# A decoder block on one core: x on the load queue, the first w_in tiles after modulation set 0, and the S5 constants begun during x

## The chip, the core and the metric

The kernel runs on one core of a Trainium2 chip. Five engines work beside each other: TensorE (PE, whose weight loads are listed apart as PEld), VectorE (DVE), ScalarE (ACT), GpSimd (POOL) and SyncE (SP), which here only issues loads. The metric is the device time of one launch in microseconds (us). Times of several launches and the trace of one profiled launch are given; in the trace every time counts from the start of its span.

## What is computed

```python
mod = silu(c) @ W_ada + b_ada           # 6 vectors: shift1, scale1, gate1, shift2, scale2, gate2
h = rms(x, norm1_w) * (1 + scale1) + shift1
u, q, k, v = split(h @ W_in)            # 256 rows of 2048; W_in has 4096 columns
y_ssm = s5_mixer(u, ...)                # 64 groups, exp/cos/sin of a*dt, a scan over 256 rows, GELU, GLU
y_att = dilated_attention(q, k, v, ...) # three branches with ALiBi, merged
x = x + gate1 * (concat(y_ssm, y_att) @ W_out)
h2 = rms(x, norm2_w) * (1 + scale2) + shift2
x = x + gate2 * ((silu(h2 @ W_gate) * (h2 @ W_up)) @ W_down)
```

x is 256 x 2048 in fp32, c one row of 2048. All weights are fp32.

## The kernel before, in words

**Weights.** Every weight tile is 128 x 1024 fp32 (0.52 MB). `load` (line 108) issues it on SP into the ring `raw`, which has 6 slots. For the matmuls on activations `ahead` (line 126) makes two tiles of it: `whi`, a copy in the reduced matmul type, cast by ACT (line 135), and `wlo`, what the cast lost, subtracted by DVE (line 137). A product takes three passes: whi with both halves of the activation and wlo with its upper half. There are 3 slots of whi and 3 of wlo (NHL = 3).

**The early stage** runs from the start to about 165 us and mixes four streams, one small step of each at a time, in the loop over `n` at the end of the printed code:

- `ada` makes the modulation vectors. Each of its first 8 sets makes two columns of shift1 and scale1 in two steps of four wada tiles: two tiles in the `raw` ring and a pair, `rawp`, in a buffer of its own. After a set ACT copies the sum (`adaev`), PE turns it into columns (`adac`, line 212), DVE makes `sh1` and `g1` (lines 216 and 218) of it, and `make_h` makes `htmp` and `hT` (lines 623 and 626) on DVE and ACT.
- `x_norm` transposes x on PE through the accumulators `uacc0` and `uacc1` (line 343) in two halves, copies them out as `xT` (line 349, one by ACT, one by DVE), squares x on ACT (line 346), and makes 1/rms on DVE and PE (line 360).
- `s5_consts` makes the constants of the SSM, well over a hundred short VectorE operations, most on 128 x 32 numbers. After it come `ssm_rot` and `ssm_tables` (four tables, m0 to m3), on DVE, ACT, PE (`wtp`, `pk`, `pk2`: lines 577, 583 and 587) and POOL.
- `unit` is the first part of h @ W_in. Unit p takes two columns of hT (set p) with three win tiles: two for u (line 639, into uacc0 and uacc1) and one for q (line 154).

**What sets the order.** SP's instructions stand in the written order. On the other engines a scheduler places the instructions; those of `make_h`, `adac` and the casts have high priority. `next(st_)` is called at steps 0 to 8, and goes through x_norm with one step of s5_consts each time; from step 9 on, `tab_step` spends a budget of 1.2 per step on what is left of `st_` and then on the tables. `ahead(NHL)` loads the first three win tiles at n == 8; after that a unit loads the next tile each time it takes one. At n == 10 SP issues `bct` (1 MB, used by the last part of the S5 constants).

ACT's queue issues `smt` (0.19 MB of small constants, among them the identity for the transposes), then x0 and x1, the halves of x (1 MB each).

Of the kernel before, what the change touches and what calls it, by code (L numbers as in the profile page):

```python
# [61 lines left out]
def body(tc, sm, tabs, bc, brow, x, wada, wg2, win, wglu, wout, wgate, wup, wdown, out):  # L62
    nc = tc.nc
    V, A, PE, G, SP = nc.vector, nc.scalar, nc.tensor, nc.gpsimd, nc.sync
# [19 lines left out]
    A.dma_start(smt, sm)  # L84
    xt = [xp.tile([128, D], F32, name=f"x{t}", tag="x", bufs=2) for t in range(2)]
    for t in range(2):
        A.dma_start(xt[t], x[t])
    col = lambda n: smt[:, COLS[n][0]:COLS[n][1]]
    ident = col("id")
    ones = const.tile([128, 128], F32, name="ones")  # L90
# [34 lines left out]
    def ahead(n, place=None):  # L125
        while len(ready) < n and order:
            raw = load(order.pop())
            if place:
                hl = place([128, 2, 2, 512], "whl", F32R)
                hi, lo = hl[:, 0], hl[:, 1]  # L130
            else:
                hi = ring.tile([128, 2, 512], F32R, name="whi", bufs=NHL)
                lo = ring.tile([128, 2, 512], F32R, name="wlo", bufs=NHL)
            with tc.high_priority(offset=HP):
                A.copy(hi, raw)  # L135
            with tc.high_priority(offset=HP2):
                V.tensor_tensor(out=lo, in0=raw, in1=hi.bitcast(F32), op=ALU.subtract)  # L137
            ready.append((hi, lo))
# [195 lines left out]
    def x_norm():  # L334

        ss1 = p1.tile([128, 2], F32, name="ss1")
        for h in range(2):
            xn = P8([128, 8, 256], f"xT{h}")
            for t in range(2):
                for i in range(2):  # L340
                    for k in range(4):
                        kc = h * 8 + i * 4 + k
                        PE.transpose(uacc[i][:, k, t * 128:(t + 1) * 128], xt[t][:, kc * 128:(kc + 1) * 128], ident)
                if h == 0:
                    junk = P8([128, D], "junk")
                    A.activation(junk, xt[t], AF.Square, accum_out=ss1[:, t:t + 1])
                    yield
            for i in range(2):
                (V.tensor_copy if i else A.copy)(xn[:, 4 * i:4 * i + 4], uacc[i])
            xnT.append(xn)  # L350
            yield
            if h == 0:
                with tc.high_priority(offset=HH):
                    V.tensor_scalar(out=ss1, in0=ss1, scalar1=1.0 / D, scalar2=EPS, op0=ALU.mult, op1=ALU.add)
                    rs1 = rsqrt(p1, ss1, 2, "a")
                    rb = ms([128, 256], "rb")
                    for t in range(2):
                        dg = T2([128, 128], "dgx")
                        V.tensor_scalar(out=dg, in0=ident, scalar1=rs1[:, t:t + 1], scalar2=None, op0=ALU.mult)
                        PE.matmul(rb[:, t * 128:t * 128 + 128], lhsT=ones, rhs=dg, start=True, stop=True)  # L360
                    A.copy(rsx, rb)
                yield
# [288 lines left out]
    def unit():  # L651
        while units:
            try:
                next(units[0])
                return
            except StopIteration:
                units.pop(0)

    def start():
        a, b = x_norm(), s5_consts()  # L660
        while next(a, 0) is None:
            next(b, None)
            yield
        yield
        yield from b

    def tabs_early():
        yield from st_
        for m in range(NTAB):
# [4 lines left out]
            yield from ssm_tables(m)  # L674

    st_ = start()
    tab_gen = tabs_early()
    U_ = []
# [13 lines left out]
    def tab_step(budget):  # L692
        debt[0] = max(debt[0] - budget, -budget)
        if debt[0] < 0:
            c_ = next(tab_gen, None)
            debt[0] += c_ or 0.0

    work = 0.0
    for n in range(66):
        next(ada)  # L700
        if n == NBC:
            SP.dma_start(bct.rearrange("p a b c -> p (a b c)"), bc)
        if n < 9:
            next(st_)
        else:
            tab_step(TB)
        if n == 8:
            ahead(NHL)
        if n >= U0:
            work += RATE  # L710
            while work >= 1.0:
                unit()
                work -= 1.0
# [548 lines left out]
def program(arrays):  # L1262
    import concourse.bacc as bacc
    nc = bacc.Bacc("TRN2", target_bir_lowering=False, num_devices=1)
    aps = {k: nc.dram_tensor(k, v.shape, F32, kind="ExternalInput").ap() for k, v in arrays.items()}
    out = nc.dram_tensor("out", (2, 128, D), F32, kind="ExternalOutput").ap()
    with tile.TileContext(nc) as tc:
        body(tc, out=out, **aps)
    return nc
# [8 lines left out]
```

## Time and profile before

| | us |
|---|---|
| launches (three) | 1246.68, 1247.48, 1251.21 |
| median | 1247.48 |
| the profiled launch | 1248.12 |
| its span in the trace | 1246.3 |
| PE busy in the span | 1193.3 (96%) |
| DVE busy | 793.3 (64%) |
| ACT busy | 572.2 (46%) |
| chain that ended last | PE 79%, DVE 10%, DMA 5%, ACT 3% |

The profiled launch is 1.82 us longer than its span. The page cuts the span into 40 slices of 31 us and gives the busy share of each engine in tenths. Here are the lines of PE, DVE, the clock that TensorE was granted and the DMA engines:

```profile
PE   4789899999998999899999999999999999999998
DVE  7964766477879998855665565565555444545544
PEclk9899999999999999899999999999999999999999
DMA  9889878897996899367777777777766656666662
```

The first column is the first 31 us. PE is below 9 tenths in four of the first five slices and in three later ones, and otherwise busy nearly all the time.

### The profile page before, as it was taken

The numbers are of one execution on the slowest core, as the hardware profiler recorded it, in microseconds if no ns is written. First come the engines' busy times: TensorE is split into PE (matmuls) and PEld (weight loads), VectorE is DVE, ScalarE is ACT, GpSimd is POOL, SyncE is SP. The second block draws the span as 40 slices with busy tenths as digits, with TensorE's granted clock in tenths as the row PEclk, the third lists the DMA queues.
The fourth block names the chain that finished last, engine by engine and source line by source line (L and its number), as shares of the span: only waits on it lengthen the run. The fifth ranks groups of instructions, "written<-read, shape, count | busy, mean of one in ns | idle before, by whom it ended". The sixth has DMA issues, their size and how long they took to land.

```text
span 1246.3 us, 17021 instructions
## 1 busy us (share of the span) xinstructions
PE 1193.3 (96%) x6312; PEld 954.0 (77%) x6312; DVE 793.3 (64%) x1402; ACT 572.2 (46%) x871; POOL 50.5 (4%) x90
## 2 busy tenths in 40 slices
PE   4789899999998999899999999999999999999998
PEld 2567667667797777688888888888888878888886
DVE  7964766477879998855665565565555444545544
ACT  3654574456455445644444444444444443434332
POOL 1110001121120000000000000000000000000000
PEclk9899999999999999899999999999999999999999
DMA  9889878897996899367777777777766656666662
GB/s 378 314 289 365 311 265 293 287 305 265 327 318 205 300 338 338 120 212 241 233 241 224 240 241 241 230 228 248 236 187 187 197 161 199 207 197 205 197 208 67
DMA packets 93906, 306.85 MB, mean 246 GB/s; under 512 B 18080, under 2 KB 20544, under 8 KB 93184
## 3 DMA queue, kind: packets, MB, share of 16 engines
q1 hardware_dynamic: 80784, 294.69, 70.7%
q0 software_dynamic: 11312, 6.70, 2.7%
q10 hardware_dynamic: 1728, 4.38, 0.9%
q8 instruction: 49, 0.80, 0.3%
q14 instruction: 33, 0.27, 0.1%
HBM read 301.54 MB, written 4.19 MB: 245 GB/s over the span
## 4 chain that ended last, share of the span: by engine, by line
PE 79%; DVE 10%; DMA 5%; ACT 3%; issue 2%; POOL 0%; DVEq 0%; ACTq 0%; POOLq 0%
PE ff L154 38%; PE dn L154 14%; PE qkv L154 8%; PE dnl L154 5%; PE ada L255 3%; DMA raw<-wada 3%; DVE wlo L137 2%; PE uacc L639 2%; PE wo L154 2%; DMA raw<-win 1%; PE y L763 1%; PE S L733 1%; DVE gate L292 1%; PE q L154 1%; DVE wkt L368 1%
## 5 line engine op out<-in xcount | busy, mean ns | idle before, releaser
L137 DVE TENSOR_TENSOR wlo<-raw,whi 128x1024 fp32r<-128x1024 f32 x365 | 446.6, 1224 | 334.5 <-ACT whi L135 333.8
L135 ACT CAST whi<-raw 128x1024 fp32r<-128x1024 f32 x365 | 384.8, 1056 | 499.3 <-PE ff L154 270.1
L154 PE MATMUL ff<-whi,h2T 128*128 128x512 f32 x1408 | 438.5, 391 | 0.7 <-DVE h2T L1074 0.5
L154 PEld LDWEIGHTS ff<-whi,h2T 128*128 128x128 f32 x1408 | 264.6, 188 | 56.6 <-ACT h2T L1073 1.0
L154 PE MATMUL ff<-wlo,h2T 128*128 128x512 f32 x704 | 274.5, 390 | 0.0
L154 PE MATMUL dn<-whi,aT 128*128 128x512 f32 x528 | 163.4, 390 | 0.0
L154 PEld LDWEIGHTS ff<-wlo,h2T 128*128 128x128 f32 x704 | 132.5, 188 | 26.9
L154 PEld LDWEIGHTS dn<-whi,aT 128*128 128x128 f32 x528 | 99.1, 188 | 21.0 <-ACT whi L135 0.2
L154 PE MATMUL qkv<-whi,hT 128*128 128x512 f32 x320 | 108.1, 405 | 0.3 <-ACT whi L135 0.2
L154 PE MATMUL dn<-wlo,aT 128*128 128x512 f32 x264 | 103.1, 391 | 0.0
L154 PEld LDWEIGHTS qkv<-whi,hT 128*128 128x128 f32 x320 | 60.6, 190 | 25.5 <-issue 6.4
L154 PE MATMUL qkv<-wlo,hT 128*128 128x512 f32 x160 | 64.1, 401 | 2.0 <-DVE wlo L137 2.0
L1132 DVE SCALAR_TENSOR_TENSOR gate<-raw,cs,gate 128x1024 f32<-128x1024 f32 x32 | 41.1, 1284 | 38.3 <-DMA raw<-wg 38.3
L639 PE MATMUL uacc<-hT,whi 128*128 128x256 f32 x256 | 51.7, 299 | 6.9 <-ACT whi L135 6.9
L154 PEld LDWEIGHTS dn<-wlo,aT 128*128 128x128 f32 x264 | 49.6, 188 | 10.8 <-issue 0.5
L154 PE MATMUL dnl<-whi,aT 128*128 128x512 f32 x176 | 54.4, 389 | 0.0
L292 DVE SCALAR_TENSOR_TENSOR gate<-raw,cs,gate 128x512 f32<-128x512 f32 x64 | 48.0, 754 | 7.6 <-DMA raw<-wada 7.2
L639 PEld LDWEIGHTS uacc<-hT,whi 128*128 128x128 f32 x256 | 42.0, 201 | 13.5 <-ACT whi L135 9.9
L255 PE MATMUL ada<-raw,c 128*4 128x256 f32 (+1 forms) x496 | 50.7, 492 | 0.0
L639 PE MATMUL uacc<-hT,wlo 128*128 128x256 f32 x128 | 38.7, 302 | 5.7 <-DVE wlo L137 5.7
L154 PEld LDWEIGHTS dnl<-whi,aT 128*128 128x128 f32 x176 | 33.0, 188 | 7.0 <-DVE o L368 0.2
L154 PEld LDWEIGHTS qkv<-wlo,hT 128*128 128x128 f32 x160 | 30.5, 191 | 8.9 <-DVE wlo L137 2.3
(318 smaller groups left out, 1257.1 us busy)
## 6 DMA issues: line engine op xcount, KB each, us to landing
raw<-wada SPq DMA_DIRECT2D x130, 512.0 KB, 5.3
raw<-wgate SPq DMA_DIRECT2D x88, 512.0 KB, 4.3
raw<-wup SPq DMA_DIRECT2D x88, 512.0 KB, 4.1
raw<-wdown SPq DMA_DIRECT2D x88, 512.0 KB, 3.7
raw<-win SPq DMA_DIRECT2D x64, 512.0 KB, 5.5
raw<-wout SPq DMA_DIRECT2D x32, 512.0 KB, 4.9
raw<-wg SPq DMA_DIRECT2D x32, 512.0 KB, 4.0
rawp<-wada SPq DMA_DIRECT2D x30, 512.0 KB, 7.2
```

Of the source, the lines that this page charges most:

```text
L135: A.copy(hi, raw)
L137: V.tensor_tensor(out=lo, in0=raw, in1=hi.bitcast(F32), op=ALU.subtract)
L154: PE.matmul(ps[t] if type(ps) is list else ps[:, t], lhsT=lhs(a, t), rhs=w[:, j], start=first and n == 0, stop=last and n == 2)
L255: PE.matmul(ps[32 * q:32 * q + 4, 0:w], lhsT=c7[:, kc, 3 - i:7 - i], rhs=wts[t][:, j * w:(j + 1) * w], start=q not in seen, stop=n == len( ...
L292: V.scalar_tensor_tensor(out=gb, in0=wt[:, j], scalar=cs[:, 2 * h + j:2 * h + j + 1], in1=gb, op0=ALU.mult, op1=ALU.add)
L368: V.tensor_tensor(out=o, in0=a, in1=b, op=op)
L639: PE.matmul(uacc[b][:, c], lhsT=wt[:, j, w], rhs=h[:, j, a], start=(kc == 0 and n == 0 and c % 2 == 0), stop=(kc == 15 and n == 2), skip_g ...
L733: PE.matmul(S[:, e, Q], lhsT=wv[:, 0, Q, e].rearrange("p i c -> p (i c)"), rhs=U[:, m, Q], start=True, stop=True)
L763: PE.matmul(y[:, Q], lhsT=Vt[:, Q, e].rearrange("p r c -> p (r c)"), rhs=hp[:, e, Q], start=False, stop=e == 1, skip_group_check=True)
L1132: V.scalar_tensor_tensor(out=g, in0=wt, scalar=cs[:, k:k + 1], in1=g, op0=ALU.mult, op1=ALU.add)
```

## The change

It moves the two loads of x from ACT's queue to the head of SP's, ahead of all weights; it calls `ahead(NHL)` at n == 4 in place of n == 8; and `start` takes two, two and one steps of s5_consts in its first three calls and none in the next six, with the rest of them from n == 9 on in `tab_step`.

```diff
     for t in range(2):
-        A.dma_start(xt[t], x[t])
+        SP.dma_start(xt[t], x[t])
@@
     def start():
         a, b = x_norm(), s5_consts()
-        while next(a, 0) is None:
-            next(b, None)
+        for i in range(9):
+            next(a, None)
+            for _ in range((2, 2, 1)[i] if i < 3 else 0):
+                next(b, None)
             yield
-        yield
         yield from b
@@
             tab_step(TB)
-        if n == 8:
+        if n == 4:
             ahead(NHL)
```

**SP, from the first wada tile on.** `raw` and `rawp` with wada are ada's tiles (four in a step, two steps in a set), those with win the tiles of unit 0. Before:

```order
L110 DMA raw_124<-wada 128x1024
L249 DMA rawp_126<-wada 128x1024 x2
L110 DMA raw_249<-wada 128x1024
L110 DMA raw_251<-wada 128x1024
L249 DMA rawp_253<-wada 128x1024 x2
L110 DMA raw_332<-wada 128x1024
L110 DMA raw_334<-wada 128x1024
L249 DMA rawp_336<-wada 128x1024 x2
L110 DMA raw_385<-win 128x1024
L110 DMA raw_391<-win 128x1024
L110 DMA raw_397<-win 128x1024
L702 DMA bct_117<-bc 128x2048
```

And now, from the head of the queue:

```order
L87 DMA x0_77<-x 128x2048
L87 DMA x1_78<-x 128x2048
L110 DMA raw_122<-wada 128x1024
L110 DMA raw_124<-wada 128x1024
L249 DMA rawp_126<-wada 128x1024 x2
L110 DMA raw_262<-wada 128x1024
L110 DMA raw_264<-wada 128x1024
L249 DMA rawp_266<-wada 128x1024 x2
L110 DMA raw_304<-win 128x1024
L110 DMA raw_310<-win 128x1024
L110 DMA raw_316<-win 128x1024
L110 DMA raw_324<-wada 128x1024
```

The three win tiles now stand ahead of set 1's first step (raw_324 and on), where they stood behind it (raw_332 to rawp_336), and bct, which followed the win tiles, follows that step. x stands ahead of everything.

**DVE, at set 0's columns.** `wlo` is unit 0's, `te` and `wkr` are the running products of the S5 constants, ss_ and el their small operands, `sh1` and `g1` the modulation columns of set 0. Before:

```order
L216 TENSOR_TENSOR sh1_103<-adac_403,smt_75 128x2
L216 TENSOR_TENSOR g1_102<-adac_403,smt_75 128x2
L368 TENSOR_TENSOR ss_td_113<-el_116 128x32
L368 TENSOR_TENSOR ss_dt_107<-el_116 128x32
L218 SCALAR_TENSOR_TENSOR g1_102<-g1_102,smt_75 128x2
L368 TENSOR_TENSOR ss_ard_108<-el_116 128x32
L371 TENSOR_SCALAR el_116<-ss_td_113 128x32
L623 SCALAR_TENSOR_TENSOR htmp_410<-xT0_146,g1_102,rsx_106 128x256 x2
L368 TENSOR_TENSOR el_116<-ss_ard_108,ss_dt_107 128x32
L371 TENSOR_SCALAR ss_tb_111<-pw_114 128x32
L368 TENSOR_TENSOR wkr_494<-te_493,el_116 128x16
L626 SCALAR_TENSOR_TENSOR hT_409<-htmp_410,sh1_103,hT_409 128x256 x2
```

Now:

```order
L368 TENSOR_TENSOR wkr_549<-te_548,el_116 128x16x16 x2
L137 TENSOR_TENSOR wlo_307<-raw_304,whi_306 128x1024
L368 TENSOR_TENSOR te_548<-wkr_549 128x8x16
L137 TENSOR_TENSOR wlo_313<-raw_310,whi_312 128x1024
L216 TENSOR_TENSOR sh1_103<-adac_347,smt_75 128x2
L216 TENSOR_TENSOR g1_102<-adac_347,smt_75 128x2
L368 TENSOR_TENSOR te_548<-wkr_549 128x8x16
L218 SCALAR_TENSOR_TENSOR g1_102<-g1_102,smt_75 128x2
L137 TENSOR_TENSOR wlo_319<-raw_316,whi_318 128x1024
L623 SCALAR_TENSOR_TENSOR htmp_354<-xT0_146,g1_102,rsx_106 128x256 x2
L368 TENSOR_TENSOR wkr_549<-te_548,el_116 128x512
L626 SCALAR_TENSOR_TENSOR hT_353<-htmp_354,sh1_103,hT_353 128x256 x2
```

Before, sh1 to hT stood in the middle of the S5 constants and ahead of every wlo. Now nearly all the S5 constants and the three wlo stand ahead of hT, and only bct follows.

**PE, at the end of unit 3 and set 4's columns.** uacc is unit 3's u part, q00 and q01 its q part, `adac_1274` the columns of set 4, on which unit 4 waits. Before:

```order
L639 MATMUL uacc1_119<-hT_847,wlo_1172 128x256
L154 MATMUL q00_120<-whi_1233,hT_847 128x512
L154 MATMUL q01_121<-whi_1233,hT_847 128x512
L212 MATMUL adac_1274<-sel_100,adaev_1243 128x2 x2
L154 MATMUL q00_120<-wlo_1234,hT_847 128x512
L154 MATMUL q00_120<-whi_1233,hT_847 128x512
L154 MATMUL q01_121<-wlo_1234,hT_847 128x512
L154 MATMUL q01_121<-whi_1233,hT_847 128x512
```

Now:

```order
L154 MATMUL q00_120<-wlo_1195,hT_784 128x512
L154 MATMUL q00_120<-whi_1194,hT_784 128x512
L154 MATMUL q01_121<-whi_1194,hT_784 128x512
L583 MATMUL pk_1218<-wst_1157,te_920 32x128 x8
L154 MATMUL q01_121<-wlo_1195,hT_784 128x512
L154 MATMUL q01_121<-whi_1194,hT_784 128x512
L587 MATMUL pk2_1228<-smt_75,te_920 128x128
L212 MATMUL adac_1274<-sel_100,adaev_1204 128x2 x2
L255 MATMUL ada_98<-rawp_1246,c7_92 4x256 x8
L255 MATMUL ada_98<-raw_1244,c7_92 4x256 x4
L255 MATMUL ada_98<-raw_1242,c7_92 4x256 x4
```

The q tile's matmuls, which followed adac_1274, now precede it, with table m3's `wtp`, `pk` and `pk2` among them. From there on both programs have the same order on PE.

## Rows read from the trace of the kernel before

**Rows 1.** Windows: us, busy us of PE, PEld, DVE, ACT, POOL (instructions), PEclk, DMA share, GB/s.

```profile
10.00:15.00 5.00, 1.94 (x8) 1.57 (x8) 4.89 (x39) 3.01 (x3) 0.95 (x1) 1.00 1.00 408
...
50.00:55.00 5.00, 4.47 (x52) 2.05 (x52) 4.80 (x16) 4.59 (x9) 0.00 (x0) 0.66 0.53 206
...
70.00:75.00 5.00, 4.33 (x46) 2.46 (x46) 5.00 (x16) 3.78 (x8) 0.00 (x0) 1.00 0.78 269
...
95.00:130.00 35.00, 34.58 (x351) 26.99 (x353) 19.30 (x56) 16.05 (x34) 1.95 (x6) 1.00 0.98 384
...
400.00:1246.00 846.00, 835.84 (x3719) 686.19 (x3717) 504.65 (x542) 361.17 (x405) 1.08 (x2) 1.00 0.68 219
```

**Rows 2.** Timeline, first 22 us: start, us, engine, line, operation, [idle before <- releaser].

```profile
5.31 0.22 ACT L182 ACTIVATE cs<-smt 128x16 f32<-128x16 f32 x1 [2.36 <-DMA smt<-sm]
...
10.22 1.91 ACT L346 ACTIVATE junk<-x 128x2048 f32<-128x2048 f32 x1 [4.70 <-DMA x<-x]
...
14.00 1.91 ACT L346 ACTIVATE junk<-x 128x2048 f32<-128x2048 f32 x1 [1.76 <-DMA x<-x]
...
15.07 1.89 PE L255 MATMUL ada<-rawp,c 128*4 128x256 f32 x16 [2.79 <-DVE ss_tb L371]
...
18.59 1.97 PE L343 MATMUL uacc<-smt,x 128*128 128x128 f32 x8
...
20.60 1.23 DVE L349 COPY xT<-uacc 128x1024 f32<-128x1024 f32 x1 [3.56 <-PE uacc L343]
...
21.88 1.75 PE L343 MATMUL uacc<-smt,x 128*128 128x128 f32 x14 [1.32 <-DVE xT L349]
```

**Rows 3.** Timeline, VectorE, 27 to 40 us.

```profile
29.64 0.88 DVE L626 SCALAR_TENSOR_TENSOR hT<-htmp,sh,hT 128x256 fp32r<-128x256 f32 x2
...
33.09 1.22 DVE L137 TENSOR_TENSOR wlo<-raw,whi 128x1024 fp32r<-128x1024 f32 x1
...
38.90 0.42 DVE L371 TENSOR_SCALAR bct<-bct 128x512 f32<-128x512 f32 x1
```

**Rows 4.** Timeline, TensorE, 34 to 58 us.

```profile
34.36 0.58 PE L639 MATMUL uacc<-hT,wlo 128*128 128x256 f32 x1 [2.87 <-DVE wlo L137]
...
45.05 1.05 PE L255 MATMUL ada<-raw,c 128*4 128x256 f32 x16
...
48.21 0.61 PE L212 MATMUL adac<-sel,adaev 128*128 128x2 f32 x4 [2.11 <-ACT adaev L267]
...
57.19 0.36 PE L639 MATMUL uacc<-hT,wlo 128*128 128x256 f32 x1
```

**Rows 5.** Timeline, TensorE, 75 to 123 us.

```profile
75.64 0.38 PE L639 MATMUL uacc<-hT,wlo 128*128 128x256 f32 x1 [0.26 <-DVE wlo L137]
...
94.77 0.66 PE L577 MATMUL wtp<-smt,wst 128*128 128x128 f32 x4 [0.44 <-ACT wv L578]
...
95.18 0.36 PE L639 MATMUL uacc<-hT,wlo 128*128 128x256 f32 x1
...
97.27 0.65 PE L583 MATMUL pk<-wst,te 128*32 128x128 f32 x16
...
104.13 0.50 PE L212 MATMUL adac<-sel,adaev 128*128 128x2 f32 x4
...
106.99 1.05 PE L255 MATMUL ada<-rawp,c 128*4 128x256 f32 x16
...
109.17 0.27 PE L639 MATMUL uacc<-hT,wlo 128*128 128x256 f32 x1
...
122.61 0.50 PE L639 MATMUL uacc<-hT,whi 128*128 128x256 f32 x2
```

**Rows 6.** Timeline, ScalarE and TensorE, 120 to 141 us.

```profile
120.47 1.05 ACT L135 CAST whi<-raw 128x1024 fp32r<-128x1024 f32 x1 [2.50 <-DMA raw<-win]
...
132.38 0.50 PE L154 MATMUL q<-wlo,hT 128*128 128x512 f32 x1 [0.81 <-DVE wlo L137]
...
140.18 0.50 PE L639 MATMUL uacc<-hT,whi 128*128 128x256 f32 x2 [1.16 <-ACT whi L135]
```

## What is forecast, before the changed kernel has run

> **What bounds the kernel now.** I read the shares first, then windows, then the timeline of the early stage, engine by engine. From 400 us on TensorE is busy for 835.84 of 846 us [rows 1]. Nothing the change touches is there: whatever the early stage wins or loses is carried to the end, unless a wait in between swallows it. The DMA engines are full between 95 and 130 us (share 0.98, 384 GB/s) but not before: 0.53 at 50 to 55 us, 0.78 at 70 to 75 us [rows 1]. So the question is when the early stage hands over at about 130 us, and who is late there.
>
> In the first 40 us the late one is VectorE: busy 4.89 of 5 us at 10 to 15 us, in 39 operations, so 0.125 us each [rows 1]. It makes the S5 constants, and sh, g, hT and wlo must fit in between. TensorE waited 2.87 us for the first wlo (34.36 us) [rows 4]. VectorE's one large hole is 3.56 us ahead of its first copy of transposed x at 20.60 us [rows 2]: the second half of x, squared from 14.00 us on, was transposed behind ada's first step, which began at 15.07 us, so these eight transposes ran at 18.59 us only.
>
> **Part by part: x on SP.** The small constants stay at the head of ACT's queue and x leaves it. At 408 GB/s [rows 1] x's 2.1 MB take 5.1 us. By 15.07 us 4.8 MB had come (smt, x, four wada tiles and some of dct), 11.7 us at that rate, so bytes flow from about 3.3 us. Behind smt and a share of dct, x0 is there by about 7.3 us and x1 by about 9.9 us, against 10.22 and 14.00 us [rows 2]. The same bytes stand ahead of ada's first step, so that still has its tiles near 15 us and gains nothing.
>
> The sixteen transposes of the first half run as soon as x lands, and VectorE's first xT copy starts at about 14 to 15 us instead of 20.60. The hole of 3.56 us goes. But the second half's transposes wait for these copies to free uacc: 16 of them, at 1.97/8 = 0.246 us when the engine came from idling and 1.75/14 = 0.125 us otherwise [rows 2], so 2.0 to 3.9 us; VectorE meets its second xT copy after 26 short operations (3.2 us) and waits there 0.6 to 1.2 us. I take a lead of 2.5 us for VectorE from there on; the bounds are 3.56 (no new wait) and 1.6 (a new wait of 2.0, all the transposes at the slow price).
>
> smt gates the first work of both ACT and VectorE; it landed at 5.31 us [rows 2]. Its bound is from there to 7.3 us (behind all of x0): 0 to +2.0. I take 0, its own row. By the Trainium skill ("DMA: Bandwidth & Descriptors", section "Queues, rings and completion order") each DMA engine goes round the queues that it has work for, one packet at a time; x's 8 KB rows now stand on the other queue in place of wada's 4 KB rows, so by that page smt would get fewer turns and land later. No row of before shows it; it is a rival below.
>
> **The S5 constants and the win tiles.** By the order, the three wlo and hT of unit 0 now stand behind nearly all S5 constants. Before, these constants ended at 38.90 us [rows 3], with everything of unit 0 ahead of them. Take off the lead of 2.5, the three wlo (3 x 1.14, an operation less what overlaps; 1.22 by its row) and sh, g, htmp and hT (1.8: two pairs of 0.88 us [rows 3] and the columns' short ones): the first wlo comes at about 31.4 us, against 33.09 [rows 3]. Then wlo, wlo, sh, g, wlo, htmp, hT, with a few constants between, take 6.2 us, and hT is done at about 37.7 us, where before it was done at 30.5 [rows 3]. So the wlo come earlier and hT 7 us later. TensorE starts unit 0 on ACT's half of hT at about 36.7 us; before it was held at 34.36 us [rows 4]. It then runs without a wait, but ada's first step of set 1 (two groups of 16 matmuls at 1.05 us [rows 4], 1.9 with their overlap; done before unit 0 until now) stands inside it. From 34.36 us to the end of set 1's second step (45.05 + 1.05 = 46.10) were 11.74 us [rows 4]; the new end is 36.7 + 11.7 + 1.9 = 50.3 us, **4.2 us later**.
>
> **What gives it back.** adac of set 1 stood at 48.21 us after waiting 2.11 us for ACT's copy [rows 4], which was queued behind table copies. Those come later now, so it follows its step by about 0.6 us: 50.9, +2.7. VectorE, early by 2.5 us, waits for it instead. Between its columns and unit 1's first wlo matmul were 9.0 us (57.19 [rows 4]), in which VectorE also made tables; about 1.1 us of those are already done by then in the new order. Unit 1: +1.6 us. Unit 2 waited for VectorE (75.64 us, wlo [rows 5]; 5.00 of 5 us busy at 70 to 75 us [rows 1]). There the new order has some 2.4 us of table work between hT and wlo in place of 4.3, so unit 2 is at +0.1 and unit 3 (95.18 [rows 5]) at -0.4 us. From this alone the change would be worth 0.4 us.
>
> **What is lost again.** At the end of unit 3 table m3's TensorE work (two wtp of 0.66, pk of 0.65 [rows 5], pk2 some 0.3: 2.25 us), whose place in unit 3 m2 has taken, stands in the q tile, and adac of set 4 stands behind all of it, no longer ahead of the q matmuls that ran after it from 104.5 to 106.99 us (2.5) [rows 5]. adac: 104.13 - 0.4 + 2.25 + 2.5 - some 0.3 (its own place) = 108.2 us, **+4.1 us**. Unit 4 depends on these columns by sh, g, htmp, hT and wlo. 5.04 us lay between adac and its first wlo matmul (109.17 [rows 5]), during which TensorE had the q tile and a step of ada to do; now it has only the ada step. Hence unit 4 at up to 113.2, +4.0. Unit 5 starts at 122.61 us [rows 5]; small waits ahead of it leave +3.2.
>
> **Who is late at 130 us.** ACT's cast at 120.47 us waited 2.50 us for its win tile, and TensorE 0.81 us at 132.38 us and 1.16 us at 140.18 us [rows 6] as a consequence: there the loads set the pace, not TensorE. These 2.0 us of waiting swallow part of the +3.2. Against that, loads slip too: ring slots held by unit 0 are freed 3 to 4 us later around 45 to 50 us, where the DMA share was already down to 0.53 (50 to 55 us [rows 1]); 0.78 at 70 us leaves room to catch up, so perhaps 1 us is left when they are full. The ends are -0.4 (all lost time swallowed) and +4.1 (none). I take +2, near the middle, since the waits of 2.0 us cover about half.
>
> **The sum.** Against the profiled launch of 1248.12 us (span 1246.3 plus 1.8), which is 0.6 us over the median: 1248.1 + 2 = **1250 us**.
>
> **Rivals.** *The lead stays (faster).* VectorE keeps the whole 3.56 us, since it is full before and after the hole, and unit 4 finds its columns in time: 1248.1 - 3.5 = 1244.6 us. For it: the hole is real, and TensorE did wait for VectorE at 34.36 us and at 75.64 us [rows 4, 5]. Against: hT now stands behind the constants. If the early win tiles also lift the dip of 0.53 (2.3 us of loads in 5), up to 5 us more could come, to about 1239.5.
>
> *Nothing happens.* x lands early, but the loads set the pace at 120 us by the same bytes in the same time, and all else is swallowed: 1248.1 us.
>
> *smt is late.* It shifts both engines' first work by up to 2 us, through the same steps: 1252 us. The page named above speaks for it; against it, smt was issued first.
>
> *Unit 0's delay stays (slower).* The win tiles of unit 2 go into ring slots that set 2's second step frees. If unit 0's 4.2 us are still there at that point, unit 2's tiles land after about 72.6 us, later than VectorE could use them; then the table work saved does not help, and the 4.2 us of unit 0 and the 4.1 us at unit 4 lie behind each other, with no slack at 120 us as the loads slip as well: 1248.1 + 8.3 = 1256.4 us. It decides by whether unit 2's first wlo matmul is later than 77 us.
>
> **How the numbers follow.** Chances: the forecast 0.42, the lead stays 0.20, nothing happens 0.15, smt late 0.10, the delay stays 0.13. The likeliest is my number, 1250 us; its own range is 1247.7 to 1252.2 (the ends above). The range to hold 8 in 10 goes down into the first rival to 1242.5, without its far end, and up to 1256, the edge of the last. A measurement of this kernel can tell about 0.5%, 6.2 us, from no change: faster is under 1241.2, slower over 1253.7. Faster then needs the lead and part of the dip: 0.08. Slower: the delay, most of it, and a rest of the smt case: 0.14. Same: 0.78.
>
> **What would show it.** Right: the first Square of x at 7 to 8 us; the xT copy at 14 to 15 us without its 3.56 us; hT of set 0 done near 37.7 us and unit 0's end near 50; unit 2's first wlo matmul between 75 and 76.5 us; adac of set 4 near 108 us and unit 4's wlo at 111 to 113 us. Wrong: smt's first user after 6.5 us; unit 0's first matmul before 34 us (then VectorE's lead is larger than I think); a first unit 4 wlo below 110 us (then adac was not binding); or the same offset at 200 us and at the end missing, which would say that the later stages are not bound by TensorE as the shares have it.

## The result and the profile after

The changed kernel takes **1257.91 us** (median of 6 launches, 1254.90 to 1260.01) against 1247.58 us for the kernel before in the same comparison: a ratio of **1.0070, with a 95% interval of 1.0047 to 1.0093**. It is slower by some 9 us (8.7 by the ratio, 10.3 by the medians); 1250 was forecast, and 1256 was the range's upper end. The profiled launch took 1258.93 us, its span 1256.9. Of the launches in the table further down two were slow, one of chg_smt_first (3065.6 us) and one of chg_h_tab_smt (1288.47 us): they are in the medians and not in the ratios.

Most of the first 30 us came as forecast. These lines of the timeline after (columns as in [rows 2]) answer to [rows 2]:

```profile
6.53 0.21 ACT L182 ACTIVATE cs<-smt 128x16 f32<-128x16 f32 x1 [4.07 <-DMA smt<-sm]
9.82 1.91 ACT L346 ACTIVATE junk<-x 128x2048 f32<-128x2048 f32 x1 [1.19 <-DMA x<-x]
...
15.79 1.21 DVE L349 COPY xT<-uacc 128x1024 f32<-128x1024 f32 x1
...
17.06 3.67 PE L343 MATMUL uacc<-smt,x 128*128 128x128 f32 x16 [5.25 <-DVE xT L349]
...
20.67 1.89 PE L255 MATMUL ada<-rawp,c 128*4 128x256 f32 x16
...
20.77 1.22 DVE L349 COPY xT<-uacc 128x1024 f32<-128x1024 f32 x1 [1.40 <-PE uacc L343]
```

x1 is there at 9.8 us in place of 14.0, and VectorE's wait of 3.56 us is gone. But smt landed at 6.53 us, not 5.31, just past the 6.5 that the prediction gives as a sign of being wrong; VectorE waits 1.40 us anew at its second xT copy; and ada's first step, now behind the second sixteen transposes, moved from 15.07 to 20.67 us. From there on, unit by unit (after, against [rows 3 to 5]):

```profile
37.76 0.80 PE L639 MATMUL uacc<-hT,whi 128*128 128x256 f32 x2 [10.11 <-ACT hT L625]
38.08 0.87 DVE L626 SCALAR_TENSOR_TENSOR hT<-htmp,sh,hT 128x256 fp32r<-128x256 f32 x2
...
53.49 0.61 PE L212 MATMUL adac<-sel,adaev 128*128 128x2 f32 x4 [0.49 <-ACT adaev L267]
...
54.13 0.16 DVE L216 TENSOR_TENSOR sh<-adac,smt 128x2 f32<-128x2 f32 x1 [4.00 <-PE adac L212]
...
71.90 1.22 DVE L137 TENSOR_TENSOR wlo<-raw,whi 128x1024 fp32r<-128x1024 f32 x1
76.24 1.22 DVE L137 TENSOR_TENSOR wlo<-raw,whi 128x1024 fp32r<-128x1024 f32 x1
...
77.94 1.05 PE L255 MATMUL ada<-rawp,c 128*4 128x256 f32 x16
...
80.15 0.58 ACT L578 COPY wv<-wtp 128x512 f32<-128x512 f32 x1 [6.69 <-PE wtp L577]
...
87.86 1.05 ACT L135 CAST whi<-raw 128x1024 fp32r<-128x1024 f32 x1
...
89.31 0.53 PE L212 MATMUL adac<-sel,adaev 128*128 128x2 f32 x4
...
114.46 0.61 PE L212 MATMUL adac<-sel,adaev 128*128 128x2 f32 x4 [0.35 <-ACT te L588]
```

The columns of sets 1, 3 and 4 (`adac`) stood at 48.21, 83.59 and 104.13 us before. They are late by 5.3, 5.7 and 10.3 us. The rows before that answer to those at 77 to 90 us, which are taken up below, are these:

```profile
71.39 1.05 PE L255 MATMUL ada<-rawp,c 128*4 128x256 f32 x16
...
82.15 1.05 ACT L135 CAST whi<-raw 128x1024 fp32r<-128x1024 f32 x1
...
83.59 0.54 PE L212 MATMUL adac<-sel,adaev 128*128 128x2 f32 x4
```

The windows (columns as in [rows 1]) show where the engines stood still:

```profile
20.00:25.00 5.00, 5.00 (x52) 2.14 (x54) 4.12 (x26) 1.47 (x3) 0.00 (x0) 1.00 0.44 154
...
30.00:35.00 5.00, 0.00 (x0) 0.00 (x0) 4.97 (x21) 0.00 (x0) 0.00 (x0) 0.50 0.99 401
...
50.00:55.00 5.00, 4.10 (x46) 2.30 (x44) 1.00 (x6) 1.61 (x3) 0.00 (x0) 1.00 0.24 68
...
95.00:130.00 35.00, 31.76 (x313) 23.71 (x312) 12.02 (x27) 14.38 (x30) 3.25 (x8) 1.00 0.88 319
...
400.00:1246.00 846.00, 838.62 (x3764) 688.45 (x3763) 512.41 (x556) 368.80 (x420) 1.08 (x2) 1.00 0.69 221
```

The load queue stalls at 20 to 25 us (154 GB/s) and at 50 to 55 us (68, before 206). TensorE does nothing from 30 to 35 us; VectorE is busy 1.00 of 5 us at 50 to 55 us, where it was busy 4.80 before: it waits for set 1's columns. From 95 to 130 us TensorE has lost 2.8 us against [rows 1], and the DMA engines are no longer full (share 0.88, before 0.98). Past 400 us both are nearly alike.

The mark for the end of the early stage is the first matmul of `qkv`, the work after the units. It ran at 171.06 us before and runs at 179.65 us now, 8.6 us later:

```profile
171.06 0.50 PE L154 MATMUL qkv<-whi,hT 128*128 128x512 f32 x1 [0.20 <-ACT whi L135]
```

```profile
179.65 0.50 PE L154 MATMUL qkv<-whi,hT 128*128 128x512 f32 x1 [0.16 <-ACT whi L135]
```

### The profile page after: what moved, and what is told of

It reads as the page before. It is cut to its first block, busy times and chain, and to the rows that moved or that the text cites. A ratio compares the mean times of both kernels' runs of the same rounds, so it can differ in the third digit from the quotient of the medians.

```text
span 1256.9 us, 17017 instructions
## 1 busy us (share of the span) xinstructions
PE 1197.6 (95%) x6312; PEld 957.7 (76%) x6312; DVE 792.8 (63%) x1402; ACT 571.0 (45%) x871; POOL 50.3 (4%) x90
## 4 chain that ended last, share of the span: by engine, by line
PE 81%; DVE 8%; DMA 5%; ACT 3%; issue 2%; SPq 0%; POOL 0%; DVEq 0%; ACTq 0%; POOLq 0%
PE ff L154 38%; PE dn L154 14%; PE qkv L154 7%; PE dnl L154 5%; PE uacc L639 3%; PE ada L255 3%; DMA raw<-wada 3%; DVE wlo L137 2%; PE q L154 2%; PE y L764 1%; DVE gate L292 1%; PE S L734 1%; PE wo L154 1%; PE atp L1155 1%; PE wtp L577 1%
```

## The experiments

Ratios are to the kernel before on the same chip; 0.001 is 1.25 us. Most launches of one kernel lie within some 3 us of their median and a few 6 us or more away, so the trace of one launch can lie that far from the median beside it: times within the early stage are read from traces, times of the whole from the medians. The last column says how much later than in the kernel before (171.06 us) the first matmul of `qkv` ran in the trace, in one launch each.

| run | median us | ratio | 95% interval | `qkv` late by, us |
|---|---|---|---|---|
| the change | 1257.91 | 1.0070 | 1.0047 to 1.0093 | 8.6 |
| x_only | 1252.63 | 1.0035 | 1.0019 to 1.0051 | 0.5 |
| win_only | 1248.91 | 1.0002 | 0.9984 to 1.0020 | -1.0 |
| start_only | 1252.91 | 1.0037 | 1.0017 to 1.0056 | 3.1 |
| x_win | 1253.57 | 1.0035 | 1.0018 to 1.0053 | 4.4 |
| chg_slots | 1258.40 | 1.0077 | 1.0053 to 1.0101 | 7.8 |
| chg_slots2 | 1255.78 | 1.0066 | 1.0044 to 1.0087 | 7.7 |
| chg_h_first | 1254.78 | 1.0062 | 1.0041 to 1.0082 | 5.9 |
| chg_catch_up | 1253.16 | 1.0042 | 1.0026 to 1.0059 | 3.8 |
| chg_all_three | 1252.62 | 1.0034 | 1.0019 to 1.0048 | 3.1 |
| chg_smt_first | 1254.89 | 1.0051 | 1.0034 to 1.0068 | 6.3 |
| x_smt_first | 1246.94 | 0.9984 | 0.9968 to 1.0001 | 1.3 |
| before_smt_first | 1247.98 | 0.9999 | 0.9982 to 1.0016 | 0.9 |
| win_smt_first | 1250.51 | 1.0016 | 1.0000 to 1.0031 | 1.7 |
| chg_h_tab_smt | 1247.30 | 0.9988 | 0.9972 to 1.0003 | 3.3 |
| chg_free_loads | 1244.86 | 0.9970 | 0.9957 to 0.9983 | -2.2 |
| chg_free_no_h | 1251.76 | 1.0017 | 0.9998 to 1.0036 | 1.5 |

### Each part alone

x_only, win_only and start_only are the three hunks of the diff, one at a time, on the kernel before; x_win is the first and the last.

> Only the two loads of x move to the head of SP's queue; the win tiles stay at n == 8 and the S5 constants are begun as before. Theory (two separate losses): x early lets VectorE run ahead, and nearly all S5 constants come to stand ahead of set 0's columns and hT, so unit 0 starts at about 38 us, set 1's second step ends 5 to 7 us later than in the kernel before, and 4 to 6 us of that reach the end: 1252 to 1254 us; the columns of set 4 have no further loss (their offset stays within 1 us of that of set 3). Rival (the win tiles moved ahead are the cause, because the third one waits for a ring slot and holds the load queue): this run is within 1.5 us of the kernel before, and its DMA share at 20 to 25 us stays at about 1.0.

> Only the first three win tiles move, to n == 4. Theory: by the order VectorE's wlo and hT of set 0 come right behind the second xT copy, so unit 0 starts before 31 us, not at 34.4, and set 1's second step ends 2 to 4 us earlier than before; some of it is swallowed where the loads set the pace (95 to 130 us): 1244 to 1247.5 us. Rival (win tiles ahead of set 1 hold the load queue): the DMA share falls well below 0.8 somewhere at 15 to 30 us, and the time is 1251 us or more.

> Only the pace of the S5 constants is changed (two, two and one steps in the first three calls, none in the next six). Theory: up to about 55 us the order and the times are those of the kernel before; the tables then come three steps later, table m3 stands in unit 3's q tile, the columns of set 4 come 4 to 5 us later, and this stays: 1251 to 1253 us. Rival (the loads at 95 to 130 us swallow it): within 1.5 us of the kernel before.

> The change without its new pace of the S5 constants. Theory: unit 0 is as late as in the change (set 1's second step ends near 53 us), but table m3 is where it was before and the columns of set 4 gain back the 4.6 us that they lost against those of set 3: 1252 to 1254.5 us, 4 to 5 us under the change. Rival (the loads are late from 20 us on, and all else only follows them): 1257 to 1258 us, as the change.

By the ratios x costs 4.4 us and the new pace of the S5 constants 4.6, and the sum is the 9 us of the change. By the ratios the win tiles cost and bring nothing: in win_only the first wlo came at 25.6 us in place of 33.09 and set 1's columns at 46.78 in place of 48.21, and at the end nothing of it was left; the gain that was expected of it did not come. The traces do not add up so neatly. At `qkv` x_only is 0.5 us late and x_win 4.4, so in these two launches the early win tiles beside x go with 3.9 us, which the ratios (1.0035 both) do not show.

The second loss is seen where it arises. In start_only the columns of set 3 stand at 83.54 us, where they stood before (83.59), and table m3 ahead of those of set 4:

```profile
106.89 0.65 PE L583 MATMUL pk<-wst,te 128*32 128x128 f32 x16
...
108.04 0.27 PE L587 MATMUL pk<-smt,te 128*128 128x128 f32 x1
108.67 0.61 PE L212 MATMUL adac<-sel,adaev 128*128 128x2 f32 x4 [0.36 <-ACT te L588]
```

That is 4.5 us after 104.13 [rows 5]. In x_win, with the old pace, set 3 is late by 5.2 us and set 4 by 3.7. The trace of x_only has set 1's columns late by 3.4 us but is only 0.5 us late at `qkv`, less than its median says.

### The table step, hT and the load queue, each mended in the change

chg_catch_up takes four steps more of the tables' generator at n = 9 to 12, chg_h_first makes the running products of the S5 constants wait for set 0's hT, and chg_slots gives the first two wada tiles a buffer of their own:

```diff
# chg_catch_up
             tab_step(TB)
+            if n < 13:
+                tab_step(TB)
# chg_h_first
+        V.tensor_copy(el[:, 0, 0, 0:1], hT[0][:, 0, 1, 0:1].bitcast(F32))
         csq(el[:, 0, 0], el[:, 0, 1], th, tmpa)
# chg_slots (chg_slots2: without "n == 0 and")
+                    if si == 0 and n == 0 and t < 2:
+                        if t == 0:
+                            pq_ = P8([128, 2, 1024], "raw0")
+                        SP.dma_start(pq_[:, t], src)
+                        wts.append(pq_[:, t])
+                        continue
```

> The change, with four more steps of the tables' generator taken at n = 9 to 12, so that table m3 stands on PE where it stood in the kernel before. Both theories: the columns of set 4 no longer lose 4.6 us against those of set 3, and it stays so: 1252 to 1254.5 us, as x_win. If instead the loads set the pace from 95 us on whatever the order: 1256.5 us or more.

> The change, with one small VectorE copy added that makes the later S5 constants (from the running products on) stand behind hT of set 0. Theory A: hT is done at 31 to 33 us in place of 39, unit 0 starts near 31 to 32 us in place of 37.8, set 1's second step ends by 48 us in place of 53; the loss at the columns of set 4 (table m3) stays: 1252 to 1254.5 us. Theory B: the load queue is held at 20 to 25 us as in the change, and the time stays at 1256.5 to 1259 us.

> The change, with the first two wada tiles in a buffer of their own in place of two ring slots, so that the third win tile needn't wait for ada's first step; the order on the other engines is that of the change. Theory A (the early loss is hT of set 0 behind the S5 constants on VectorE): the DMA dip at 20 to 25 us (154 GB/s in the change) fills to over 350 GB/s, but unit 0 still starts near 38 us, set 1's second step still ends near 53 us, and the time is that of the change within 1.5 us: 1256.5 to 1259 us. Theory B (the early loss is the load queue held by the ring): the 1.3 MB not lost are worth 3 us at 400 GB/s and reach the end: 1253 to 1255.5 us.

> The change, with the first two wada tiles of both steps of set 0 in buffers of their own in place of ring slots: the load queue then waits for no ring slot before set 1's second step, and the DMA share stays near 1.0 from 5 to 35 us. Theory A (hT of set 0 behind the S5 constants, not the loads, makes unit 0 late): unit 0 still starts at 37 to 39 us and the time is that of the change within 1.5 us: 1256.5 to 1259.5 us. Theory B (the 1.3 to 1.5 MB that the queue loses at 20 to 30 us reach the end): 3 us less, 1253.5 to 1255.5 us.

> The change with all three: own buffer for the first two wada tiles, hT of set 0 ahead of the running products, and the tables caught up. If A, B and the table step are all the loss there is, this is at or under the kernel before: 1243 to 1249 us. If the later landing of the small constants (1.2 us) or anything else is left over: 1249.5 to 1252 us.

The table step gives back 3.5 us by the ratios, as expected, and 4.8 us at `qkv`; the intervals just touch, and start_only shows the same loss by itself. In chg_h_first hT begins at 31.7 us and set 1's columns stand at 48.4 us, but table m3 holds those of set 4 again. The end gains 1 us by the ratios and 3 by the medians, within the intervals, and `qkv` 2.7 us in the one trace: undecided here.

chg_slots was no test. Its DMA dip only moved from 20 to 25 us on to 25 to 30 us (first two lines), and in chg_slots2, where neither step of set 0 uses the ring, to 30 to 35 us (the other lines):

```profile
20.00:25.00 5.00, 3.81 (x45) 1.88 (x47) 3.94 (x22) 1.01 (x1) 0.95 (x1) 1.00 0.86 342
25.00:30.00 5.00, 2.42 (x36) 1.18 (x31) 5.00 (x49) 3.48 (x5) 0.00 (x0) 1.00 0.52 164
```

```profile
25.00:30.00 5.00, 1.54 (x24) 0.73 (x12) 5.00 (x50) 2.61 (x4) 0.97 (x1) 1.00 1.04 421
30.00:35.00 5.00, 0.00 (x0) 0.00 (x0) 4.96 (x21) 0.00 (x0) 0.00 (x0) 0.51 0.40 140
50.00:55.00 5.00, 4.10 (x46) 2.30 (x44) 0.95 (x6) 1.61 (x3) 0.00 (x0) 1.00 0.22 62
```

By 55 us as many bytes are missing as in the change (17.2 MB have come in both, 19.0 before), and neither run is faster by more than its interval. The ring is full because its readers are late. In the change SP issued the second of these two loads only at the end of the row, at 52.95 us:

```profile
45.73 7.22 SPq L110 DMA_DIRECT2D raw<-wada  x2
```

By then ada's second step of set 1 (51.95 to 53.0 us), which stands behind unit 0 on TensorE, had begun to free its slots. The stall follows from the late unit, and more slots move it only.

### What was left: smt's landing

chg_all_three had all three mends and was still 4 us over the kernel before. So smt was moved to the head of SP's queue, ahead of x where x stands there:

```diff
-    A.dma_start(smt, sm)
+    SP.dma_start(smt, sm)
```

> The change, with the small constants (smt) moved from ACT's queue to the head of SP's, ahead of x. smt lands at 3 to 4 us in place of 6.5. Theory (VectorE's sum of work is what the early stage follows, so each us of its start counts): unit 0 starts 2 to 3 us earlier than in the change (35 to 36 us) and the end follows by 1.5 to 3 us: 1254.5 to 1256.5 us. Rival (only the order of hT and table m3 counts, the start is swallowed later): 1257 to 1259 us.

> As x_only (x at the head of SP's queue, win tiles and S5 constants as before), with smt ahead of x in the same queue. smt lands at 3 to 3.5 us in place of 6.6. If smt's landing is worth what it was worth in the change (1254.9 against 1257.9): 1249 to 1250.5 us, and what is left over the kernel before (0.5 to 2 us) is hT behind the S5 constants. If the 4.4 us of x_only are all hT's place: 1251.5 to 1253.5 us.

> The kernel before, with smt alone moved to the head of SP's queue; x stays on ACT's. smt lands at 3 to 4 us in place of 5.3. Theory (VectorE's start counts): 1.5 to 2.5 us are won: 1246 to 1247.5 us. Rival (what is won is swallowed where the loads set the pace, or the ada tiles behind it lose as much): 1248 to 1249.5 us.

> The kernel before with the first three win tiles at n == 4 (as win_only, which measured as before) and smt at the head of SP's queue; x stays on ACT's. Theory (VectorE's start counts): 1.5 to 3 us under win_only: 1245.5 to 1247.5 us, which would be the fastest so far. Rival (swallowed where the loads set the pace): 1248 to 1249.5 us.

> The change with hT of set 0 ahead of the running products, the tables caught up, and smt at the head of SP's queue (ada's first two tiles in the ring again). Theory (what was left over in chg_all_three, some 4 us, is smt's later landing and VectorE's later start): 1247 to 1249.5 us. Rival (it is something else that x on SP brings): 1251 to 1253 us as in chg_all_three.

smt's first reader on VectorE, in x_only, in x_smt_first and in before_smt_first, shows when it landed:

```profile
6.61 0.18 DVE L189 TENSOR_REDUCE sel<-smt 128x4 f32<-128x16 f32 x1 [4.78 <-DMA smt<-sm]
```

```profile
3.14 0.18 DVE L189 TENSOR_REDUCE sel<-smt 128x4 f32<-128x16 f32 x1 [1.31 <-DMA smt<-sm]
```

```profile
6.53 0.18 DVE L189 TENSOR_REDUCE sel<-smt 128x4 f32<-128x16 f32 x1 [4.70 <-DMA smt<-sm]
```

With smt first and x behind it in one queue, x_only loses all its 4.4 us by the ratios (and 2 more, within the interval). The traces do not show where: `qkv` came at 171.60 us in x_only and at 172.38 in x_smt_first, though smt landed 3.5 us earlier there. In the change smt first gains 2.4 us by the ratios, whose intervals overlap, and 2.3 us at `qkv`.

The two runs without x on SP were meant to land smt earlier and landed it later (6.53 and 6.05 us), since x stayed on the other queue. So they show the reverse: in before_smt_first smt came 1.2 us later than in the kernel before, as late as in the change, and the ratio is 0.9999 (0.9982 to 1.0016). There a landing that late costs no more than 2 us, so the 4.4 us of x_only are not shown to be smt's landing. hT also stands later in both (36.52 us in x_only, 34.35 in x_smt_first, 29.64 before), and no run put hT first beside x alone.

chg_h_tab_smt is where chg_all_three was not: level with the kernel before. It differs in two things, smt's place and the ring slots of ada's first two tiles, which are back in the ring. Against the change its interval is clear (0.9972 to 1.0003, against 1.0047 to 1.0093): smt, the tables and hT mended together take away the whole loss at the end, though `qkv` is still 3.3 us late in its one trace.

### With all of it mended, and one taken out again

chg_free_loads is chg_h_tab_smt with the buffers of chg_slots2; chg_free_no_h is that without the copy that puts hT first.

> As chg_h_tab_smt (hT first, tables caught up, smt at the head of SP's queue), and the first two wada tiles of both steps of set 0 in buffers of their own. Theory A: there VectorE's order is mended, and the loads are what is left; at 50 us 1.3 MB more have come, of which some 2 us reach the end: 1244 to 1246.5 us. Rival (the ring is full again at 45 us and the bytes are lost there instead): 1246.5 to 1249 us, as chg_h_tab_smt.

> As chg_free_loads (smt at the head of SP's queue, tables caught up, set 0's first tiles in buffers of their own), but with set 0's hT behind the S5 constants as in the change. Theory A (hT's place makes unit 0 late, and it follows through the ring): hT near 35 us in place of 28.7, set 1's columns 4 us later, and 3 us or more of it reach the end: 1247.5 to 1250 us. Rival (only smt's landing and the tables count, hT's place is swallowed by unit 2): 1244 to 1246.5 us, as chg_free_loads.

chg_free_loads is faster than both kernels, by 0.17 to 0.43% against the one before. Without hT first it loses 5.9 us (1.0017 against 0.9970, the intervals apart); 3.7 us of it are there at `qkv`. hT begins at 27.78 us in the first and at 36.12 in the second:

```profile
27.78 0.89 DVE L633 SCALAR_TENSOR_TENSOR hT<-htmp,sh,hT 128x256 fp32r<-128x256 f32 x2 [0.18 <-ACT hT L632]
```

```profile
36.12 0.87 DVE L632 SCALAR_TENSOR_TENSOR hT<-htmp,sh,hT 128x256 fp32r<-128x256 f32 x2
```

And the loads at 45 to 50 us, in the first and in the second:

```profile
45.00:50.00 5.00, 3.24 (x23) 1.93 (x26) 4.68 (x17) 3.66 (x7) 0.00 (x0) 0.57 0.79 320
```

```profile
45.00:50.00 5.00, 5.00 (x49) 3.62 (x52) 2.12 (x8) 1.24 (x2) 0.00 (x0) 1.00 0.08 33
```

The same buffers, and 320 GB/s become 33; by 50 us 19.0 MB had come in the first and 16.9 in the second. Only the copy that puts hT first was taken out, and the loads followed.

## Why the prediction was wrong

**The lead of VectorE (taken 2.5 us, bounds 1.6 to 3.56): wrong in size.** 3.56 us did go. But smt came 1.2 us later (6.53 against 5.31), which I had as a rival and put at 0 in the sum, and the new wait was 1.40, not 0.6 to 1.2. That leaves 0.96 us, below my lower bound. hT then ended at 38.95 us, not 37.7. I had given the slow price of a transpose, 0.246 us, to an engine that comes from idling; [rows 2] does not show that, since those eight ran without a wait behind ada's step, and in the change sixteen took 3.67 us, 0.23 each.

By the Trainium skill ("DMA: Bandwidth & Descriptors", section "Queues, rings and completion order") a DMA engine takes the queues in turn, a packet at a time. The traces agree in the outcome: smt landed later (6.0 to 6.8 us against 5.1 to 5.3) wherever x's large rows stood on the other queue. That rule spoke against the change, and I gave it one chance in ten.

**Unit 0's delay (forecast 4.2 us): right in mechanism, too small.** ada's second step of set 1 ended at 53.0 us, not 50.3, so 6.9 us late. Of the 2.7 us beyond the forecast 1.25 are hT's; most of the rest goes with TensorE's clock, which I had left as it was. TensorE had no work for 10.11 us, its granted clock was 0.50 from 30 to 40 us (the 1.2 GHz level), and unit 0 ran its first 5.5 us at the slow pace, before some 3: 2.5 us more at half the speed cost about 1.2.

**What gives it back (forecast: unit 1 at +1.6, unit 2 at +0.1, unit 3 at -0.4 us): the step that failed first.** set 1's columns came 5.3 us late (forecast 2.7), and VectorE stood still for 4.00 us ahead of them. Unit 1's first wlo matmul ran at 61.99 us, 4.8 us late (forecast 1.6). Unit 1's wlo were late from the first (60.73 us, 55.72 before) to the last (71.90, 65.49 before), with VectorE full again. Unit 2's first wlo came at 76.24 us, only 1.9 us late: the shorter table work ahead of it was real (2.3 us between hT and wlo, 2.4 forecast). But I had followed VectorE alone. On TensorE ada's step of set 3 and the table's `wtp` stand behind unit 1's last tile: 77.94 us, 71.39 before, so 6.5 us late. ACT waited 6.69 us for that wtp, and its cast for unit 2's second tile, in line behind the copies of the table, came at 87.86 us, 82.15 before. So set 3's columns are late by 5.7 us. This is my slower rival, "unit 0's delay stays", in its outcome and nearly in its time (1256.4 us), but not in its mechanism: the cast of unit 2's first tile ran at 72.43 us without a wait, and the second's stood behind the table's copies and not behind its load. The mark that I set for it was met: unit 2's first wlo matmul ran at 81.20 us, past 77 (75.64 in [rows 5]), since that table work stands ahead of it too. So the failed step is this: I took the delay of unit 0 to be given back by VectorE's shorter work, -0.4 us at unit 3, and TensorE's and ACT's order handed it on: unit 3's first wlo matmul came at 100.92 us, 5.7 us late. In the prediction's own terms the offsets of units 2 and 3 were not worked out either: 1.6 less the table work saved (4.3 less 2.4) is -0.3 us, not 0.1.

**Table m3 (forecast +4.1 at set 4's columns): right.** set 4 lost 4.6 us against set 3 in the change and 4.5 in start_only. Only the base was wrong: I counted it from -0.4, it was +5.7. Unit 4's first wlo matmul came 10.6 us late, at 119.79 (109.17 before; forecast 4.0).

**Half of it swallowed at 120 to 141 us: right in size, partly by luck.** From unit 4's first wlo matmul to `qkv` the lateness shrank from 10.6 to 8.6 us: 2.0 us, as forecast, though from a far larger loss. Of the two waits of TensorE that I had counted in [rows 6] one gave. The 0.81 us at 132.38 us are gone: the same matmul ran at 141.68 us without a wait. That fits the loads as its cause, for ACT's wait for a win tile ahead of it shrank from 2.50 to 0.80 us. The other came back unchanged (first row), 9.3 us later than at 140.18 us in [rows 6]:

```profile
149.45 0.51 PE L639 MATMUL uacc<-hT,whi 128*128 128x256 f32 x2 [1.16 <-ACT whi L135]
150.71 0.39 PE L639 MATMUL uacc<-hT,wlo 128*128 128x256 f32 x1 [0.64 <-DVE wlo L137]
153.82 1.05 PE L255 MATMUL ada<-rawp,c 128*4 128x256 f32 x16 [0.21 <-DMA rawp<-wada]
```

It belongs to the order on ACT, whose cast stands behind other work there, and not to the loads; a wait of that kind takes nothing in. In its place ada's wait for its own load shrank, from 0.84 us before to 0.21 (last row). I had not counted that one; it and the 0.81 us are 1.4 of the 2.0 us.

**What stays open.** The shares don't add up. hT's place is worth 5.9 us with the rest mended, and 1 to 3 us, within the intervals, in the change; smt's landing 2.4 us in the change, and what it is worth in x_only is not shown. Each mend moves VectorE, the ring and TensorE's clock, and which of them then ends last was not taken apart further.

The end of one trace says less than its early stage. Matched matmul by matmul, the change is 8.6 us behind the kernel before from 171 to 220 us and 10.6 from 540 us on, and the distance moves only in between. There TensorE's granted clock, as the mean of a window, fell in other places: before it was 0.96 at 220 to 260 us and 0.91 at 480 to 520 us, after 0.96 at 260 to 300 us and 0.83 at 380 to 400 us. The launches point the same way: of 31 launches of the kernel before, measured beside x_only, the eight with a mean granted clock of 0.986 or less took 1249.98 us in the middle, the eleven with 0.990 or more 1248.46. So part of the scatter, and of the differences of one or two us between medians, goes with the clock. Why it falls in other places each time stays open.

## What to carry to other kernels

A wait on one engine is worth its length only if what that engine does with the time is what others wait for; ask of an engine that gets ahead what it will take first, and look in the order for the short, wanted work that now stands behind long, unhurried work. A wait that a later stage shows is slack only if its cause comes from outside the delayed chain, as the waits for loads did here; if the chain carries its own waits with it, they move along and swallow nothing. And when a large load changes queues, ask what small load on the other queue everybody's first instruction waits for.

## What the runs showed of the hardware

smt (0.19 MB) lands by what the *other* queue holds. Issued first in all of these runs, it was there at 3.0 to 3.3 us with x behind it in its own queue (3.14 in x_smt_first), at 5.1 to 5.3 with the 4 KB rows of wada on the other queue (the kernel before, win_only, start_only), and at 6.0 to 6.8 with the 8 KB rows of x on the other queue, whichever of the two queues that was: 6.53 both in the change, with smt on ACT's, and in before_smt_first, with smt on SP's. Whether it is the size of the rows or of the loads that counts, no run separates.
